# Feed-forward layers of a hybrid decoder: gated features kept in their accumulator copies, one tile in place of four, and earlier first loads for summed weights

## The chip, the cores and the metric

One Trainium2 chip, one core. The metric is the device time of one execution in microseconds (us), the median of repeated runs. The core has a matmul engine (TensorE, called PE in the profile; its weight loads are PEld), a vector engine (VectorE, DVE), an activation engine (ScalarE, ACT), GpSimd (POOL, which here issues the accumulating DMAs) and SyncE (SP, which issues the plain DMA loads). Each engine runs its own queue in order.

## What is computed

512 tokens of width 1024 go through two layers, a gated-MLP mixer in the first and retention in the second, each followed by the same kind of feed-forward layer (hidden width 2816). The change touches the feed-forward layers and the order of some loads elsewhere:

```python
def swiglu(h, w_gu, w_down):
    a, b = jnp.split(h @ w_gu, 2, axis=-1)
    return (jax.nn.silu(a) * b) @ w_down

def reference(...):
    h = x
    for i in range(DEPTH):                       # DEPTH = 2
        hn = rmsnorm(h, mix_norm_g[i])
        h = h + (sgu_mixer(hn, ...) if i % 2 == 0 else retention(hn, ...))
        h = h + swiglu(rmsnorm(h, ffn_norm_g[i]), ffn_w_gu[i], ffn_w_down[i])
    return rmsnorm(h, final_norm_g)
```

## The kernel before

**Arithmetic.** Every float32 operand is split in a high and a low part, `h` and `l`, of the matmul's own type; a product is three matmuls (`three`, L243 to L246). ACT makes the high part of a weight tile (`high`, L213), DVE the low part (`low`, L220). So each weight tile of 128 by 1024 has three buffers in its life: `wr` (raw, from the DMA), `wh` and `wl`.

**Seven products.** Large matrix products are done in blocks of two by two with seven block products in place of eight (`seven`, L313). They are called P1, P7, P6, Q4, P5, P2 and P3; in the feed-forward units and in small down projections their order is `LATER`: P1, P7, P6, P2, P5, Q4, P3. Some need a sum of several weight blocks. A sum is made on DVE (`plus`, L364), or by the DMA: the first block is loaded by SP (`load`, L333), and the others are added to it in place by accumulating DMAs that POOL issues (`add`, L336). For products named in `dma` the whole sum is made so; for products in `onto` the last block is added to the finished tile of the product before.

**A feed-forward layer** (`feed_forward`, L1003). First `project_t("gl...")` makes the last two of the 22 feature tiles (gates and values) with plain products; `first_evac` (L1016) applies silu to the gates and multiplies by the values. Then five `unit`s make four feature tiles each. In a unit, ACT copies three accumulators out of PSUM: `s1` after P1, `y7` after P7, `u2` after P6 (`copy`, L1028). After P2 and Q4 the gates `s1` and `u2` are completed and go through silu; `product` (L1032) multiplies them by the values, `y7` and the accumulator of P3. The results of units 0 to 3 go to tiles `hq[u][0]` and `hq[u][1]` of their own; those of unit 4 go to four tiles `he`, whose third slice already holds the two features of `gl` since the beginning of the layer. Down projections follow: `dn_0` after units 0 and 1, `dn_1` after unit 4 (`into_x`, L494). Where a down projection is small (`dn_0`: 14 steps) P7 and P5 are in `dma`, Q4 is in `onto`; `dn_1` has 28 steps, P7 in `dma`, P6 and Q4 in `onto`.

**Buffers.** Nearly all tiles, raw weights, their parts and the features, come from one pool `gen` of `N_GEN = 38` buffers of equal size (`G`, L123). A load or a result that finds none free waits until the last reader of one has finished.

**Order.** `pipeline` (L89) calls the preparations of a job a fixed number of jobs ahead: plain loads `FETCH = 8`, sums on DVE `SUM = 7`, high parts `HIGH = 6`, low parts `PREP = 5`. For a sum made by DMA the accumulating DMAs go `ADD = 8` jobs ahead (`STEP = 3` more for each further block) and the first load `LOAD` jobs ahead of the first of them. One job of a down projection is 12 matmuls, one of a unit 24 shorter ones. A scheduler then lays the engines' queues out, by this order as priority, and gives out the buffers.

```python
            if p in dma:
                n = len(bs) - 1
                return [(ADD + STEP * (n - 1) + LOAD, first)] + [
                    (ADD + STEP * (n - 1 - i), lambda b=b: add(p, b, g, s, nk)) for i, b in enumerate(bs[1:])]
```

Of the kernel before, what the change touches and what calls it, by code (L numbers as in the profile page):

```python
# [8 lines left out]
F32 = mybir.dt.float32  # L9
F32R = mybir.dt.float32r  # L10
I32 = mybir.dt.int32
AF = mybir.ActivationFunctionType
ALU = mybir.AluOpType
PSUM = bass.MemoryType.PSUM

P = 128
# [10 lines left out]
FETCH = 8  # L27
ADD = 8
STEP = 3
LOAD = 2  # L30
HIGH = 6
SUM = 7
N_GEN = 38
# [75 lines left out]
def trunk(ctx, tc, x, positions, mix_g, ffn_g, fin_g, sgu_w_in, sgu_w_s, sgu_b_s, sgu_ln_g, sgu_ln_b,  # L109
          sgu_w_out, ret_w_in, ret_gn_g, ret_w_out, ffn_w_gu, ffn_w_down, invf, decay, out):  # L110
    nc = tc.nc
# [9 lines left out]
    H = T // 2  # L121

    def G(name, dtype=F32, shape=(P, 2, T)):  # L123
        return gen.tile(list(shape), dtype, tag="g", name=name)
# [188 lines left out]
    def seven(name, w, groups, c1, c2, A, evac, mid=None, look=3, turned=False, order=ORDER, dma=(), onto=()):  # L313
# [21 lines left out]
        def add(p, b, g, s, nk):  # L335
            nc.gpsimd.dma_start(raw[p, 0, g, s][:, 0:nk, :], source(b, g, s, nk), accum_op=ALU.add)  # L336

        def fetch(p, g, s, nk):
# [10 lines left out]
# [4 lines that stand above are left out]
# [90 lines left out]
    def rows(k0, n):  # L443

        return [(list(range(k0, k0 + n // 2)), list(range(k0 + n // 2, k0 + n)))]
# [295 lines left out]
    def xA(name):  # L741

        made = {}

        def qr(i, j):
            return XR[name, i][j]

        s1 = []

        def A(p, g=0, ask=False):  # L750
            if p in ("P1", "P2", "Q4"):
                i, j = {"P1": (0, 0), "P2": (0, 1), "Q4": (1, 1)}[p]
                return tuple(xn[q][:, 4 * j:4 * j + 4, i * H:(i + 1) * H] for q in "hl")
            if p not in made:
                sign = -1.0 if p in ("P5", "P3") else 1.0
                h, l = (G(f"x{p}{q}_{name}", F32R, (P, 4, H)) for q in "hl")
                if p == "P6":
                    A("P5")
                elif p == "P3":
                    A("P6")  # L760
                s = G(f"x{p}_{name}", F32, (P, 4, H)) if p in ("P7", "P5") else s1[0]
                if p == "P5":
                    s1.append(s)

                def total():
                    a, b, op = {"P7": (qr(0, 0), qr(1, 0), ALU.subtract), "P5": (qr(1, 0), qr(1, 1), ALU.subtract),
                                "P6": (s, qr(0, 0), ALU.subtract), "P3": (s, qr(0, 1), ALU.add)}[p]
                    nc.vector.tensor_tensor(s, a, b, op)

                def high():  # L770
                    nc.scalar.activation(h, s, AF.Copy, scale=sign)

                def low():
                    nc.vector.scalar_tensor_tensor(l, s, sign, f32(h), ALU.mult, ALU.subtract)
                made[p] = Chain(total, high, low), (h, l)
            chain, hl = made[p]
            if not ask:
                chain.finish()
            return hl
        return A  # L780
# [222 lines left out]
    def feed_forward(l, ready):  # L1003

        w = ffn_w_gu[l]
        hq = [[None, None] for _ in range(5)]
        he = []
        gates = [None] * 5

        def hidden(u, i):  # L1010
            gates[u].finish()
            return hq[u][i]

        xparts = xA(f"f{l}")

        def first_evac(ps):  # L1016
            sl = G(f"silu{l}_l")
            nc.scalar.activation(sl, ps[0], AF.Silu)
            he.extend([[G(f"he{l}_{a}_{i}", F32, (P, 4, H)) for i in range(2)] for a in range(2)])
            for a in range(2):  # L1020
                for i in range(2):
                    hs = slice(i * H, (i + 1) * H)
                    nc.vector.tensor_tensor(he[a][i][:, 2, :], sl[:, a, hs], ps[1][:, a, hs], ALU.mult)

        def unit(u, mid=None):
            st_ = {}

            def copy(key, src):  # L1028
                st_[key] = G(f"{key}_{l}_{u}", F32, (P, 4, H))
                nc.scalar.activation(st_[key], src, AF.Copy)  # L1030

            def product(i, r, g, parts):  # L1032
                for ms, part in parts:
                    dst = he[part][i][:, 0:2, :] if u == 4 else hq[u][i][:, ms, :]
                    nc.vector.scalar_tensor_tensor(dst, r[:, ms, :], -1.0, g[:, ms, :], ALU.mult, ALU.mult)

            def evac(p, acc, c):
                if p == "P7":
                    copy("y7", acc["Y"])
                    if u < 4:  # L1040
                        hq[u] = [G(f"h{l}_{u}_{i}", F32, (P, 4, H)) for i in range(2)]
                elif p == "P1":
                    copy("s1", acc["X"])
                elif p == "P6":
                    copy("u2", acc["X"])
                elif p in ("Q4", "P2"):
                    a, ps = (st_["u2"], acc["Y"]) if p == "Q4" else (st_["s1"], acc["Z"])
                    gates[u] = Chain(lambda: nc.vector.tensor_tensor(a, a, ps, ALU.add),
                          lambda: nc.scalar.activation(a, a, AF.Silu),
                          *([lambda: product(1, st_["y7"], a, [(slice(0, 2), 0), (slice(2, 4), 1)] if u == 4 else [(slice(0, 4), 0)])] if p == "Q4" else []))  # L1050
                elif p == "P5":
                    nc.vector.tensor_tensor(st_["y7"], st_["y7"], acc["X"], ALU.add)
                elif p == "P3":
                    product(0, acc["X"], st_["s1"], [(slice(2 * c, 2 * c + 2), c)])
            seven(f"gu{l}_{u}", w, rows(0, KD), u * T, FF + u * T, xparts, evac, mid, turned=True, order=LATER, dma=("P7",), onto=("Q4",))

        t = [list(range(4 * u, 4 * u + 4)) for u in range(5)]
        A = [combos(f"h{l}_0", lambda g, i, j: hidden(j, i), (4,)),
             combos(f"h{l}_1", lambda g, i, j: he[j][i][:, 0:3, :] if g else hidden(2 + j, i), (4, 3))]

        project_t(f"gl{l}", w, ((20 * P, 2 * P), (FF + 20 * P, 2 * P)), first_evac, halves=True,
                  mid={("h", 0): lambda: xparts("P5", ask=True), ("h", 1): lambda: xparts("P7", ask=True), ("h", 2): lambda: xparts("P6", ask=True),
                       ("h", 3): lambda: xparts("P3", ask=True)})
        unit(0)
        unit(1, {("P2", 1): lambda: A[0]("P1", 0, ask=True), ("P5", 0): lambda: A[0]("P7", 0, ask=True), ("P3", 1): lambda: A[0]("P6", 0, ask=True)})
        into_x(f"dn{l}_0", ffn_w_down[l], [(t[0], t[1])], A[0])
        unit(2, {**{(p, 0): turn_tables for p in LATER}, ("P3", 1): turn_tables} if l == 0 else None)
        unit(3)
        unit(4, {("P2", 1): lambda: A[1]("P1", 0, ask=True), ("P5", 0): lambda: A[1]("P7", 0, ask=True), ("P3", 1): lambda: A[1]("P6", 0, ask=True)})
        into_x(f"dn{l}_1", ffn_w_down[l], [(t[2], t[3]), ([16, 17, 20], [18, 19, 21])], A[1], ready, look=5)  # L1070


    feed_forward(0, normed("r", mix_g[1:2], raw_copy("r")))

    xparts = xA("r")
# [147 lines left out]


    feed_forward(1, finish)
    pipeline(jobs)

# [32 lines left out]
```

## Time and profile before

| what | value |
| --- | --- |
| median of 3 runs | 1236.56 us (1231.20 to 1238.92) |
| the profiled execution's own time | 1234.63 us |
| its span, first to last instruction | 1232.7 us |
| granted TensorE clock, mean | 0.994 |
| PE / DVE / ACT / POOL busy | 1198.5 / 919.9 / 629.2 / 137.5 us |
| DMA | 204.87 MB, mean 166 GB/s |

The profile is of one execution; 1.9 us of its time lie outside the span. Busy time says how full an engine is, not whether it sets the end: for that the waits, the chain of work that ended last and the windows are read.

### The profile page before, as it was taken

To read this page: it belongs to the slowest core of one execution; us is meant where nothing else is said; L and a number is where in the kernel's file an instruction comes from. 1 tells how busy PE (TensorE), PEld (TensorE's weight loads), DVE (VectorE), ACT (ScalarE), POOL (GpSimd) and SP (SyncE) were. 2 spreads that over 40 slices of the span, in tenths; PEclk is the share of its full clock that TensorE was granted. 3 is DMA by queue.
4 is the path that set the end of the run, shared out by engine and by line. 5 is a ranking of instruction groups with operands and counts; after the bars stand their busy time and mean duration, and the time that the engine had idled before them with its cause. 6 is when DMAs were issued, how large, how long until landed. Compare 5 with 4: busy or idle time off the path is not lost.

```text
span 1232.7 us, 18012 instructions
## 1 busy us (share of the span) xinstructions
PE 1198.5 (97%) x7230; PEld 1071.5 (87%) x7230; DVE 919.9 (75%) x1105; ACT 629.2 (51%) x782; POOL 137.5 (11%) x125
## 2 busy tenths in 40 slices
PE   8999999998999999999999999999999989999996
PEld 7888899996999987888888888887899979999875
DVE  6385587687987698996665757779786778666887
ACT  7323365444544546655454646556654554455454
POOL 1000001111101120101101011220001011100310
PEclk9999999999999999999999999999999999999999
DMA  9323327678867987566566467896556678677982
GB/s 336 109 69 102 95 69 188 165 162 204 197 149 178 230 166 254 153 153 169 130 167 132 128 167 153 178 192 216 137 137 148 178 206 201 155 190 191 173 236 84
DMA packets 112995, 204.87 MB, mean 166 GB/s; under 512 B 7144, under 2 KB 20496, under 8 KB 112912
## 3 DMA queue, kind: packets, MB, share of 16 engines
q1 hardware_dynamic: 83088, 146.56, 37.0%
q0 software_dynamic: 29824, 57.18, 28.4%
q8 instruction: 56, 0.92, 0.3%
q14 instruction: 27, 0.22, 0.1%
HBM read 201.61 MB, written 2.10 MB: 165 GB/s over the span
## 4 chain that ended last, share of the span: by engine, by line
PE 83%; DMA 6%; DVE 5%; issue 3%; POOL 1%; ACT 1%; SPq 0%; DVEq 0%; POOLq 0%; ACTq 0%
PE X_gu L245 6%; PE X_gu L246 6%; PE X_gu L244 6%; DMA wr_dn_P<-in_ffn_w_down 4%; PE Y_gu L245 3%; PE Y_gu L244 3%; PE Y_gu L246 3%; PE X_vg L244 2%; PE X_vg L245 2%; PE ps_qk L246 2%; PE ps_qk L245 2%; PE ps_qk L244 2%; PE X_vg L246 2%; PE X_dn L245 2%; PE X_dn L244 2%
## 5 line engine op out<-in xcount | busy, mean ns | idle before, releaser
L213 ACT ACTIVATE wh_gu_P<-wr_gu_P 128x1024 fp32r<-128x1024 f32 x120 | 124.2, 1054 | 83.5 <-DMA wr_gu_P<-in_ffn_w_gu 33.8
L220 DVE TENSOR_TENSOR wl_gu_P<-wr_gu_P,wh_gu_P 128x1024 fp32r<-128x1024 f32 x120 | 145.2, 1219 | 21.2 <-ACT wh_gu_P L213 21.0
L213 ACT ACTIVATE wh_dn_P<-wr_dn_P 128x1024 fp32r<-128x1024 f32 x72 | 69.4, 982 | 71.5 <-DMA wr_dn_P<-in_ffn_w_down 37.6
L336 POOL DMA_DIRECT2D wr_gu_P<-in_ffn_w_gu x40 | 48.2, 1237 | 478.4 <-DMA wr_gu_P<-in_ffn_w_gu 148.0
L220 DVE TENSOR_TENSOR wl_dn_P<-wr_dn_P,wh_dn_P 128x1024 fp32r<-128x1024 f32 x72 | 79.8, 1128 | 14.4 <-ACT wh_dn_P L213 11.7
L220 DVE TENSOR_TENSOR wl_vg_P<-wr_vg_P,wh_vg_P 128x1024 fp32r<-128x1024 f32 x48 | 58.2, 1219 | 24.9 <-ACT wh_vg_P L213 19.9
L364 DVE TENSOR_TENSOR wr_gu_P<-wr_gu_P,wr_gu_P 128x1024 f32<-128x1024 f32 x40 | 48.6, 1221 | 31.2 <-DMA wr_gu_P<-in_ffn_w_gu 30.9
L336 POOL DMA_DIRECT2D wr_dn_P<-in_ffn_w_down x36 | 41.5, 1210 | 183.3 <-DVE wl_dn_P L220 78.5
L213 ACT ACTIVATE wh_vg_P<-wr_vg_P 128x1024 fp32r<-128x1024 f32 x48 | 49.7, 1055 | 20.1 <-PE X_vg L245 10.7
L336 POOL DMA_DIRECT2D wr_vg_P<-in_ret_w_in x24 | 28.9, 1294 | 265.6 <-DVE wl_qk L220 58.3
L244 PE MATMUL ps_qk<-XH_r,wh_qk 128*128 128x512 f32 (+1 forms) x160 | 55.3, 349 | 0.5 <-ACT XH_r L706 0.5
L245 PE MATMUL ps_qk<-XL_r,wh_qk 128*128 128x512 f32 (+1 forms) x160 | 55.5, 348 | 0.0
L246 PE MATMUL ps_qk<-XH_r,wl_qk 128*128 128x512 f32 (+1 forms) x160 | 55.3, 348 | 0.0
L244 PE MATMUL X_gu<-XH_f,wh_gu_P 128*128 128x256 f32 x160 | 45.4, 284 | 0.5 <-ACT xr_f L738 0.5
L245 PE MATMUL X_gu<-XL_f,wh_gu_P 128*128 128x256 f32 x160 | 45.3, 283 | 0.0
L246 PE MATMUL X_gu<-xP6h_f,wl_gu_P 128*128 128x256 f32 x160 | 45.3, 283 | 0.0
L245 PE MATMUL X_gu<-xP5l_f,wh_gu_P 128*128 128x256 f32 x160 | 45.3, 283 | 0.0
L245 PE MATMUL X_gu<-xP6l_f,wh_gu_P 128*128 128x256 f32 x160 | 45.3, 283 | 0.0
L244 PE MATMUL X_gu<-xP5h_f,wh_gu_P 128*128 128x256 f32 x160 | 45.3, 283 | 0.0
L246 PE MATMUL Y_gu<-XH_f,wl_gu_Q 128*128 128x256 f32 x160 | 45.3, 283 | 0.0
L246 PE MATMUL X_gu<-XH_f,wl_gu_P 128*128 128x256 f32 x160 | 45.3, 283 | 0.0
L244 PE MATMUL Z_gu<-XH_f,wh_gu_P 128*128 128x256 f32 x160 | 45.3, 283 | 0.0
(513 smaller groups left out, 4193.3 us busy)
## 6 DMA issues: line engine op xcount, KB each, us to landing
wr_gu_P<-in_ffn_w_gu SPq DMA_DIRECT2D x100, 512.0 KB, 4.5
wr_dn_P<-in_ffn_w_down SPq DMA_DIRECT2D x50, 512.0 KB, 5.3
wr_gu_P<-in_ffn_w_gu POOLq DMA_DIRECT2D x40, 512.0 KB, 6.8
wr_vg_P<-in_ret_w_in SPq DMA_DIRECT2D x40, 512.0 KB, 4.5
wr_dn_P<-in_ffn_w_down POOLq DMA_DIRECT2D x30, 512.0 KB, 7.6
wr_vg_P<-in_ret_w_in POOLq DMA_DIRECT2D x24, 512.0 KB, 6.3
wr_ro_P<-in_ret_w_out SPq DMA_DIRECT2D x20, 512.0 KB, 4.7
wr_qk<-in_ret_w_in SPq DMA_DIRECT2D x32, 256.0 KB, 3.1
```

The lines of the kernel that those rows point to most:

```text
L213: nc.scalar.activation(h, s, AF.Copy)
L220: nc.vector.tensor_tensor(l, s, f32(h), ALU.subtract)
L244: nc.tensor.matmul(o, ah, bh, start=start, stop=False, skip_group_check=True)
L245: nc.tensor.matmul(o, ah, bl, start=False, stop=False, skip_group_check=True)
L246: nc.tensor.matmul(o, al, bh, start=False, stop=stop, skip_group_check=True)
L336: nc.gpsimd.dma_start(raw[p, 0, g, s][:, 0:nk, :], source(b, g, s, nk), accum_op=ALU.add)
L364: nc.vector.tensor_tensor(a, a, b, ALU.add)
```

## The change

Three edits. `LOAD` goes from 2 to 3: the first load of every sum that the DMA makes goes out three jobs ahead of its first accumulating DMA. The results of units 0 to 3 are written over `y7` and `s1`, so `hq` has no tiles of its own. And `first_evac` writes one tile `hf` with a single multiply; the four `he` tiles are made only after P5 of unit 4 (`gather`), where ACT copies four slices of `hf` into them.

```diff
-LOAD = 2
+LOAD = 3
@@ feed_forward
+        first = []
         def first_evac(ps):
             sl = G(f"silu{l}_l")
             nc.scalar.activation(sl, ps[0], AF.Silu)
+            e = G(f"hf{l}")
+            nc.vector.tensor_tensor(e, sl, ps[1], ALU.mult)
+            first.append(e)
+
+        def gather():
+
             he.extend([[G(f"he{l}_{a}_{i}", F32, (P, 4, H)) for i in range(2)] for a in range(2)])
             for a in range(2):
                 for i in range(2):
-                    hs = slice(i * H, (i + 1) * H)
-                    nc.vector.tensor_tensor(he[a][i][:, 2, :], sl[:, a, hs], ps[1][:, a, hs], ALU.mult)
+                    nc.scalar.activation(he[a][i][:, 2, :], first[0][:, a, i * H:(i + 1) * H], AF.Copy)
@@ unit, evac
                 if p == "P7":
                     copy("y7", acc["Y"])
-                    if u < 4:
-                        hq[u] = [G(f"h{l}_{u}_{i}", F32, (P, 4, H)) for i in range(2)]
+                    hq[u][1] = st_["y7"]
                 elif p == "P1":
                     copy("s1", acc["X"])
+                    hq[u][0] = st_["s1"]
...
                 elif p == "P5":
                     nc.vector.tensor_tensor(st_["y7"], st_["y7"], acc["X"], ALU.add)
+                    if u == 4:
+                        gather()
```

## Rows read from the trace of the kernel before

**Rows 1.** The page's first part: busy time, share, instructions of each engine.

```profile
PE 1198.5 (97%) x7230; PEld 1071.5 (87%) x7230; DVE 919.9 (75%) x1105; ACT 629.2 (51%) x782; POOL 137.5 (11%) x125
```

**Rows 2.** Waits of PE, whole span: total us, times, longest.

```profile
PE Y_dn L244 <- ACT h_Q4h L479: 9.1, 2, 4.8
PE X_dn L245 <- DVE wl_dn_P L220: 2.9, 4, 0.9
...
PE X_ro L244 <- ACT z_P5h L479: 2.6, 1, 2.6
```

**Rows 3.** Windows: busy PE, PEld, DVE, ACT, POOL, granted clock, DMA share, GB/s.

```profile
290.80:296.80 6.00, 6.00 (x20) 4.67 (x21) 6.00 (x6) 4.81 (x5) 1.19 (x1) 0.73 0.87 310
...
1013.70:1019.70 6.00, 5.88 (x18) 4.43 (x19) 6.00 (x6) 4.60 (x5) 1.19 (x1) 0.72 0.94 314
...
464.00:478.00 14.00, 11.07 (x45) 8.34 (x46) 12.99 (x14) 9.56 (x15) 0.00 (x0) 1.00 0.76 252
1180.00:1201.00 21.00, 18.79 (x80) 14.60 (x79) 16.61 (x17) 10.88 (x16) 0.00 (x0) 1.00 0.90 267
520.00:820.00 300.00, 300.00 (x1426) 252.26 (x1425) 214.06 (x261) 162.90 (x224) 39.70 (x33) 1.00 0.65 150
```

**Rows 4.** The chain that ended last, first layer's `dn_0`: start, us, what.

```profile
266.10 0.23 PE X_dn L244
...
267.23 8.04 DMA wr_dn_P<-in_ffn_w_down
...
276.86 9.02 DMA wr_dn_P<-in_ffn_w_down
```

**Rows 5.** Timeline of ACT in `dn_0` of either layer.

```profile
285.91 1.06 ACT L213 ACTIVATE wh_dn_P<-wr_dn_P 128x1024 fp32r<-128x1024 f32 x1 [8.22 <-DMA wr_dn_P<-in_ffn_w_down]
...
1008.79 1.06 ACT L213 ACTIVATE wh_dn_P<-wr_dn_P 128x1024 fp32r<-128x1024 f32 x1 [8.73 <-DMA wr_dn_P<-in_ffn_w_down]
```

**Rows 6.** Waits of the SP queue, 243 to 270 us.

```profile
SPq L333 <- DVE wr_dn_P L364: 16.9, 2, 13.7
...
SPq L333 <- PE X_dn L246: 4.0, 1, 4.0
```

**Rows 7.** Timeline of the SP queue, end of its long wait.

```profile
258.62 0.37 SPq L333 DMA_DIRECT2D wr_dn_P<-in_ffn_w_down  x1
```

**Rows 8.** DMA, 243 to 262 us: busy tenths in 40 slices; issues, median us to landing.

```profile
DMA  0000769899999999970294999970000000137992
...
wr_dn_P<-in_ffn_w_down POOLq DMA_DIRECT2D x2, 512.0 KB, 6.5
```

**Rows 9.** Groups by shape: busy us, mean ns of one, idle before.

```profile
L1035 DVE SCALAR_TENSOR_TENSOR h<-y,u 128x1024 f32<-128x1024 f32 x8 | 9.8, 1224 | 9.3 <-ACT u L1049 5.6 <-PE X_dn L245 3.7
...
L1023 DVE TENSOR_TENSOR he<-silu_l,ps_gl 128x256 f32<-128x256 f32 x8 | 2.9, 416 | 2.4 <-PE ps_gl L246 1.3 <-ACT silu_l L1018 1.1
...
L1048 DVE TENSOR_TENSOR u<-u,Y_gu 128x1024 f32<-128x1024 f32 x10 | 12.1, 1214 | 0.0
...
L1131 ACT ACTIVATE sh<-s 128x256 fp32r<-128x256 f32 x4 | 1.6, 400 | 0.0
```

**Rows 10.** Waits of the SP queue, 400 to 432 us.

```profile
SPq L333 <- DVE wl_dn_P L220: 24.9, 1, 24.9
```

**Rows 11.** Timelines around `dn_1` of the first layer: ACT, POOL, DVE, PE.

```profile
427.87 1.06 ACT L213 ACTIVATE wh_dn_P<-wr_dn_P 128x1024 fp32r<-128x1024 f32 x1 [6.00 <-DMA wr_dn_P<-in_ffn_w_down]
...
425.82 1.19 POOL L336 DMA_DIRECT2D wr_dn_P<-in_ffn_w_down  x1 [3.78 <-DMA wr_dn_P<-in_ffn_w_down]
...
452.75 1.82 DVE L220 TENSOR_TENSOR wl_dn_P<-wr_dn_P,wh_dn_P 128x1024 fp32r<-128x1024 f32 x2
...
454.77 0.39 PE L245 MATMUL X_dn<-wl_dn_P,h_P6h 128*128 128x512 f32 x1
```

**Rows 12.** Timelines in the first retention head: DVE, then PE.

```profile
538.53 1.22 DVE L220 TENSOR_TENSOR wl_vg_P<-wr_vg_P,wh_vg_P 128x1024 fp32r<-128x1024 f32 x1
...
542.72 0.39 PE L245 MATMUL X_vg<-wl_vg_P,xP6h_r 128*128 128x512 f32 x1
```

## The prediction

> **What bounds the kernel now.** I read the page's busy times first: PE is busy 97% of the span [rows 1]. Of the 1232.7 us, 34.2 are left, so this edit of buffers and loads can only win PE's idle time, and what the clock loses after it. The waits of PE say where that is [rows 2]: the two longest, 9.1 us together, are in `dn_0`, one in each layer; then come small ones in `dn_1` (2.9 in four pieces), one in the retention's output projection (2.6) and the start. Between 520 and 820 us, the retention heads, PE has no idle time [rows 3].
>
> Next, what ends the long wait. The chain through `dn_0` of the first layer [rows 4] runs: SP issues a load at 267.23 that lands after 8.04 us; POOL's accumulating DMA onto it goes out at 276.86 and takes 9.02; ACT, which stood idle 8.22 us for exactly that landing [rows 5], makes the high part of this P5 weight, then those of Q4, then `h_Q4h`, and PE starts again. The second layer does the same (8.73 us on ACT [rows 5]). So PE waits for a sum that started too late. Why late: SP's queue had stood 13.7 us on one buffer whose last reader was a DVE sum [rows 6], until 258.62 [rows 7], and then 4.0 us more on one that a PE product of the same stage held [rows 6]. From 243 to 262 us the DMA engines have nearly empty stretches [rows 8]: there is bandwidth, there are no buffers. The pool of 38 is the bound behind the bound.
>
> After each of these waits PE runs for a while at the lower of its two clock levels: the granted clock is 0.73 over 6.0 us in one layer, 0.72 in the other [rows 3], a mean of the half level (1.2 GHz) and the full one (2.4 GHz). That loses (1 - 0.73) x 6 + (1 - 0.72) x 6 = 3.3 us. After the small waits of `dn_1` the clock stays 1.00 [rows 3].
>
> **The change, part by part.**
>
> *One tile `hf` in place of four `he`.* From the end of `gl` to P5 of unit 4, so through units 0 to 3 and `dn_0`, three more buffers are free. SP takes whatever is free for the next load in its queue. Before, the loads behind the 13.7 us wait are P2's first, P5's first, P2's second and P5's second (the late one, fourth). With three more buffers, three of them need not wait for the releases that they waited for.
>
> *`LOAD` 3.* The P5 and P7 loads move up one job, 12 x 0.23 = 2.7 us in a down projection [rows 4]; the adds stay at 8 jobs. In SP's order the second P5 load passes the second P2 load, so the late load becomes the third of the four, and the three new buffers reach it. It can then leave between the start and the end of that long wait, 244.9 to 258.6 us, in place of 267.23. Even at 258.6, with the 8.04 and 9.02 us of [rows 4] and 1.6 us between, its sum is complete at 277.3, 8.6 us ahead of 276.86 + 9.02 = 285.88. That is more than the 4.8 us that PE waited. I count both waits and both spells of low clock as gone: 9.1 + 3.3 = 12.4 us.
>
> *Results over `y7` and `s1`.* No instruction is added or removed. The two tiles live on as features where two new ones did, so what is saved is one buffer for the time of a product, and the wait for it: DVE stood idle 3.7 us in two places before `h<-y,u` for a buffer that a PE product of `dn_0` held [rows 9]. Neither wait reaches PE; it goes at zero, with 3.7 us as its upper end if DVE is late in `dn_0` afterwards.
>
> *What it adds.* In `first_evac`, four multiplies of 0.416 us become one, by the nearest shape (PSUM source, 1024 wide) 1.21 us [rows 9]: 0.45 us less on DVE in each layer, worth nothing at a point with no PE wait. In `gather`, four ACT copies of 256 columns, 0.40 us each by a copy of the same size [rows 9]: 1.6 us of ACT in each layer, beside the last products of unit 4, where ACT stands idle 6.00 us for a landing [rows 11]. Hidden; uncovered it would be 2 x 1.6 = 3.2 us. Its other price is buffers: four at once, while SP already waits 24.9 us for one [rows 10]. Behind a copy that waits stand ACT's high parts for `dn_1`, and behind those DVE and PE. Bounds: nothing, if the scheduler finds four released together; the rival below, if not. I take nothing net, since P7's loads for `dn_1` also leave earlier, and their adds go out as soon as they land (POOL [rows 11]).
>
> *`LOAD` elsewhere.* In each unit and retention head a P7 load now stands ahead of P1's first in SP's queue. Where buffers are short that costs P1 one turn; in the units the three buffers pay for it, in the heads nothing does. The tightest head weight I found has 542.72 - (538.53 + 1.22) = 3.0 us between its low part and its use [rows 12], about one job. I take 0; the bounds are a gain of the 2.6 us of the output projection [rows 2] and a loss of one job less that margin in four heads, near 0, or 2.7 in one if it has no margin.
>
> *What is late next.* With the wait gone, DVE's work in `dn_0` is pressed into less time, as in `dn_1`, where PE loses 2.9 and 2.2 us in small pieces [rows 3]. `dn_0` has half the steps and fewer sums in a row; I take 0.5 us a layer, 1.0 in all, with 0 and 5.1 as ends.
>
> Sum: 12.4 - 1.0 = 11.4 us. The profiled execution took 1234.63 us, so its like would take 1223.2; the median of the runs is 1.93 higher, so 1236.56 - 11.4 = 1225.2: I say **1225**.
>
> **The rivals.**
>
> *The buffers go elsewhere.* High and low parts and feature parts ask for buffers too. If they take the three, only the one job of `LOAD` is left: 4.8 - 2.7 and 4.3 - 2.7 remain, 3.7 us, without low clock: 12.4 - 3.7 = 8.7 us, 1228. If the scheduler's order on POOL also puts the two Q4 adds ahead, the whole wait may stay: 1236. Middle 1231. For it: SP's waits show a pool that is never free. Against: SP takes a load as soon as one is.
>
> *More than forecast.* The earlier P7 sums start the sequence P7, P6, Q4 of `dn_1` sooner, and its 2.9 + 2.2 us go as well: 1236.56 - 12.4 - 5.1 = 1219. For it: the adds follow the landing of the loads [rows 11]. Against: DVE is busy 12.99 of 14 us there [rows 3].
>
> *Earlier loads slow the adds.* Accumulating DMAs of the same size land in 6.5 us in a window with empty stretches [rows 8] and in 9.02 beside more loads [rows 4]. If the loads that moved up sit beside P7's adds, these land 2.5 us later. `dn_0` bears that; in `dn_1` DVE ends a pair of low parts at 454.57 and PE uses the first at 454.77 [rows 11], 0.8 us after that first one ended, so 1.7 us would show in each layer: 1225 + 3.4, about 1229. The Trainium skill, "DMA: Bandwidth & Descriptors", section "Issuing engines are not separate DMA queues", speaks for this rival: DMAs started by different engines run on the same 16 DMA engines and interleave, so an earlier start on one queue is paid by the other. By that rule the trace agrees that adds slow down in company, but the empty stretches of [rows 8] are where the loads would move to.
>
> *Slower than before: `gather` holds ACT.* The four copies sit in ACT's queue at P5 of unit 4 and wait for buffers while three early loads that nobody needs yet hold theirs. SP's wait there was 24.9 us for one buffer [rows 10]; if ACT waits half of that, 12 us, less 2 us of margin (0.8 in the tightest place, 3 elsewhere), PE loses 10 us in each layer and the low clock comes back there, 3.3: 23.3 - 12.4 gives 1247. It decides from 12.4 / 2 + 2 = 8 us of wait a layer. Against it: these copies come earlier in the program than the later loads of `dn_1`, and so go before them where a buffer is given out.
>
> **How the numbers follow.** Forecast 0.48 (1225, its own range 1220 to 1229); buffers elsewhere 0.24 (1228 to 1236); more than forecast 0.15 (1219); adds slowed 0.04 (1229); `gather` 0.09 (1240 to 1250). About 1% (12.4 us) is what a measurement of this kernel can tell from no change; by chance the terms of the sum come to just that. Faster by more needs under 1224.2: the 1219 case and some four tenths of the forecast, 0.35. Slower by more needs over 1248.9: half of the last rival, 0.05. The rest 0.60. The range 1218 to 1237 leaves out most of the last rival and the edge of the 1219 case, under 2 in 10.
>
> **What would show it.** In the profile after: the two waits of PE before `Y_dn` gone from its list and no clock below 1.00 in `dn_0`; SP's load for the second P5 sum leaving before 260 us and its add landing before PE reaches P2's end; ACT idle before that high part under 2 us; `dn_1`'s waits still near 2.9 and 2.2. If PE still waits in `dn_0` for the same landing, the buffers went elsewhere; if waits appear on ACT before the copies of `hf`, and on PE at the start of `dn_1`, `gather` took the gain. The forecast is wrong above all if the scheduler lays the queues out in a way that the old trace doesn't suggest, since every queue is laid out anew.

## The result, and the profile after

| | median us | runs | range | profiled execution, its span |
|---|---|---|---|---|
| before | 1235.32 | 6 | 1231.20 to 1238.92 | 1234.63, 1232.7 |
| after | 1220.03 | 6 | 1218.24 to 1221.26 | 1218.24, 1216.5 |

The ratio is 0.9879, with a 95% interval of 0.9855 to 0.9903: 15.3 us less by the medians, 16.2 by the two spans, where 11.4 were forecast. The time lies within the range given. Of the three chances it is "faster by over 1%" that the median falls into (the interval just reaches across), the case that had been given 0.35.

First the page's busy times and PE's waits over the whole span, which answer [rows 1] and [rows 2]:

```profile
PE 1192.5 (98%) x7230; PEld 1068.3 (88%) x7230; DVE 919.7 (76%) x1099; ACT 629.6 (52%) x790; POOL 137.4 (11%) x125
```

```profile
PE X_dn L245 <- DVE wl_dn_P L220: 3.1, 4, 1.1
PE X_ro L244 <- ACT z_P5h L479: 2.7, 1, 2.7
```

The 9.1 us before `Y_dn` are no longer in the list. What is left in the forecast's places is DVE's low parts in `dn_1` and the retention's output projection, which kept its 2.7. Where the time came from is seen from three windows, one a stage: first layer's FFN, retention with its output projection, second layer's FFN. Before, then after (length, then PE's busy time and the other engines'):

```profile
157.60:500.30 342.70, 334.37 (x2359) 313.84 (x2358) 278.86 (x305) 177.55 (x200) 44.45 (x38) 1.00 0.72 180
500.30:872.10 371.80, 368.07 (x1787) 310.26 (x1786) 277.70 (x343) 207.37 (x287) 43.37 (x37) 1.00 0.66 163
872.10:1224.00 351.90, 342.34 (x2375) 319.60 (x2373) 266.14 (x279) 178.33 (x201) 42.67 (x37) 0.99 0.68 168
```

```profile
157.20:491.50 334.30, 332.03 (x2358) 312.93 (x2357) 278.65 (x302) 177.57 (x204) 44.71 (x38) 1.00 0.73 185
491.50:863.50 372.00, 368.18 (x1787) 310.33 (x1786) 278.32 (x343) 207.66 (x287) 43.22 (x36) 1.00 0.66 162
863.50:1207.90 344.40, 340.05 (x2375) 318.76 (x2373) 265.20 (x277) 178.37 (x205) 42.40 (x36) 1.00 0.68 171
```

The retention is as long as it was. The two FFNs are 8.4 and 7.5 us shorter, in two ways: PE's idle time (length less busy time) falls from 8.3 to 2.3 and from 9.6 to 4.4, 11.3 together; and PE's busy time, for the same matmuls, falls by 2.3 in each, 4.6 together. The second is for the most part the clock (3.5 of the 4.6, worked out further down): in either layer one spell at the lower level is gone, as the windows over `dn_0` show (they answer the first two of [rows 3]; the sixth number is the granted clock), with `dn_1` of either layer under them:

```profile
283.80:289.80 6.00, 6.00 (x29) 4.95 (x28) 6.00 (x7) 3.19 (x3) 1.99 (x2) 1.00 1.01 240
1001.00:1007.00 6.00, 6.00 (x28) 4.96 (x27) 5.11 (x5) 3.07 (x3) 1.71 (x2) 1.00 0.88 157
450.00:464.00 14.00, 12.90 (x57) 10.17 (x56) 10.32 (x11) 5.50 (x6) 0.00 (x0) 1.00 0.94 279
1162.00:1183.00 21.00, 20.12 (x88) 15.98 (x86) 17.12 (x17) 10.89 (x15) 1.55 (x2) 1.00 0.92 271
```

In six microseconds of `dn_0` PE now does 29 matmuls where it did 20. In `dn_1` PE's single waits add up to 1.6 us in the first layer and 1.4 in the second, where they were 2.9 and 2.2: the ones before `Y_dn` are gone there as well.

Now the chain that the forecast was about, on its three queues in the first layer's `dn_0`. SP's waits from 243 to 270 us answer [rows 6], and the load of P5's second sum [rows 4]; then POOL's accumulating DMAs and ACT, which answer [rows 4] and [rows 5]:

```profile
SPq L333 <- DVE h_P7l L483: 10.8, 1, 10.8
SPq L333 <- PE Y_gu L246: 5.6, 1, 5.6
SPq L333 <- DVE y L1041: 3.6, 1, 3.6
```

```profile
258.43 0.76 SPq L333 DMA_DIRECT2D wr_dn_P<-in_ffn_w_down  x1
```

```profile
256.33 1.19 POOL L336 DMA_DIRECT2D wr_dn_P<-in_ffn_w_down  x1 [12.24 <-DMA wr_dn_P<-in_ffn_w_down]
265.38 1.22 POOL L336 DMA_DIRECT2D wr_dn_P<-in_ffn_w_down  x1 [7.86 <-DVE h_S L457]
267.10 2.43 POOL L336 DMA_DIRECT2D wr_dn_P<-in_ffn_w_down  x2 [0.51 <-issue]
```

```profile
272.66 1.99 ACT L213 ACTIVATE wh_dn_P<-wr_dn_P 128x1024 fp32r<-128x1024 f32 x2
274.55 1.04 ACT L479 ACTIVATE h_P5h<-h_S 128x1024 fp32r<-128x1024 f32 x1
275.50 1.04 ACT L213 ACTIVATE wh_dn_Q<-wr_dn_P 128x1024 fp32r<-128x1024 f32 x1
278.01 1.07 ACT L213 ACTIVATE wh_dn_Q<-wr_dn_P 128x1024 fp32r<-128x1024 f32 x1 [1.47 <-DMA wr_dn_P<-in_ffn_w_down]
278.98 1.04 ACT L479 ACTIVATE h_Q4h<-y 128x1024 fp32r<-128x1024 f32 x1
```

The load leaves at 258.43 instead of 267.23. Its add goes out at 265.38, is complete at 272.85 and makes nobody wait: both high parts of P5 follow each other at 272.66. `h_Q4h` is ready at 280.0, where it was ready at 290.8. Two things are not as forecast. SP's longest wait is still 10.8 us where it was 13.7, though the first load behind it leaves at 252.07 where it was 258.62. And POOL's queue has another order: P5's second add now stands ahead of the two adds of Q4 (the pair at 267.10), where it stood behind them.

### The profile page after: what moved, and what is told of

Same layout as the page of the kernel before. It is cut to its first block, busy times and chain, and to the rows that moved or that the text cites. A ratio compares the mean times of both kernels' runs of the same rounds, so it can differ in the third digit from the quotient of the medians.

```text
span 1216.5 us, 18009 instructions
## 1 busy us (share of the span) xinstructions
PE 1192.5 (98%) x7230; PEld 1068.3 (88%) x7230; DVE 919.7 (76%) x1099; ACT 629.6 (52%) x790; POOL 137.4 (11%) x125
## 4 chain that ended last, share of the span: by engine, by line
PE 87%; DVE 4%; issue 3%; DMA 3%; POOL 1%; ACT 1%; SPq 0%; DVEq 0%; POOLq 0%; ACTq 0%
PE X_gu L246 6%; PE X_gu L245 6%; PE X_gu L244 6%; PE Y_gu L246 3%; PE Y_gu L244 3%; PE Y_gu L245 3%; PE X_vg L244 2%; PE ps_qk L246 2%; PE ps_qk L245 2%; PE X_vg L246 2%; PE X_vg L245 2%; PE ps_qk L244 2%; PE X_dn L245 2%; PE X_dn L246 2%; PE X_dn L244 2%
## 5 line engine op out<-in xcount | busy, mean ns | idle before, releaser
L220 DVE TENSOR_TENSOR wl_gu_P<-wr_gu_P,wh_gu_P 128x1024 fp32r<-128x1024 f32 x120 | 144.9, 1219 | 38.7 <-ACT wh_gu_P L213 38.6
L220 DVE TENSOR_TENSOR wl_vg_P<-wr_vg_P,wh_vg_P 128x1024 fp32r<-128x1024 f32 x48 | 58.2, 1219 | 25.9 <-ACT wh_vg_P L213 20.7
L336 POOL DMA_DIRECT2D wr_vg_P<-in_ret_w_in x24 | 28.8, 1219 | 265.0 <-DVE sl L1140 59.7
L220 DVE TENSOR_TENSOR wl_gu_Q<-wr_gu_P,wh_gu_Q 128x1024 fp32r<-128x1024 f32 x20 | 24.4, 1222 | 28.9 <-ACT wh_gu_Q L213 28.9
L244 PE MATMUL Y_gu<-xP7h_f,wh_gu_P 128*128 128x256 f32 x160 | 45.3, 283 | 0.0
L245 PE MATMUL Y_gu<-xP7l_f,wh_gu_P 128*128 128x256 f32 x160 | 45.3, 283 | 0.0
L246 PE MATMUL Y_gu<-xP7h_f,wl_gu_P 128*128 128x256 f32 x160 | 45.3, 283 | 0.0
L244 PE MATMUL X_gu<-xP6h_f,wh_gu_P 128*128 128x256 f32 x160 | 45.3, 283 | 0.0
```

Source lines behind the costliest of these rows:

```text
L220: nc.vector.tensor_tensor(l, s, f32(h), ALU.subtract)
L244: nc.tensor.matmul(o, ah, bh, start=start, stop=False, skip_group_check=True)
L245: nc.tensor.matmul(o, ah, bl, start=False, stop=False, skip_group_check=True)
L246: nc.tensor.matmul(o, al, bh, start=False, stop=stop, skip_group_check=True)
```

## The experiments

Each run has its time and ratio against the kernel before on the same chip. Totals hide which stage moved, so the table also has the lengths of three stages in the profiled execution: from the first `ps_gl` to the first `ps_qk`, from there to the second layer's first `ps_gl`, and from there to PE's last instruction. Between 371.8 and 373.8 in the middle column only a spell of low clock or a small wait around the output projection differs. In the last column most executions have such a spell near 890 us, at the stage's start, and five of those with `hf` have none (LOAD 2, add three jobs late, not in place, P5's add held, 37 buffers); it makes 1.5 us (PE's busy time from there to `dn_0` is 110.3 us with it and 108.8 without).

| kernel | median us | ratio (95%) | FFN 1 | retention | FFN 2 |
|---|---|---|---|---|---|
| before | 1235.32 | 1 | 342.7 | 371.8 | 351.9 |
| after | 1220.03 | 0.9879 (0.9855 to 0.9903) | 334.4 | 372.0 | 344.4 |
| LOAD 3 only | 1223.84 | 0.9900 (0.9880 to 0.9919) | 336.0 | 373.1 | 346.8 |
| hf and gather only | 1225.47 | 0.9919 (0.9899 to 0.9939) | 339.3 | 371.9 | 350.7 |
| in place only | 1232.17 | 0.9969 (0.9956 to 0.9983) | 340.5 | 373.1 | 350.4 |
| after, LOAD 2 | 1223.58 | 0.9903 (0.9883 to 0.9924) | 335.8 | 373.3 | 344.3 |
| LOAD 3 for P5 only | 1224.74 | 0.9913 (0.9899 to 0.9926) | 337.3 | 373.1 | 346.3 |
| LOAD 3, add three jobs late | 1234.34 | 0.9987 (0.9973 to 1.0000) | 341.6 | 376.6 | 346.5 |
| after, add three jobs late | 1223.15 | 0.9898 (0.9883 to 0.9913) | 337.0 | 374.6 | 344.5 |
| after, not in place | 1220.03 | 0.9875 (0.9860 to 0.9889) | 335.5 | 373.1 | 344.4 |
| LOAD 3, P5's add held behind Q4's | 1229.44 | 0.9961 (0.9947 to 0.9975) | 336.4 | 378.5 | 347.0 |
| after, P5's add held behind Q4's | 1226.54 | 0.9937 (0.9922 to 0.9953) | 335.5 | 378.1 | 345.2 |
| after, LOAD 4 | 1224.90 | 0.9920 (0.9904 to 0.9936) | 335.4 | 377.3 | 345.0 |
| after, 37 buffers | 1220.72 | 0.9902 (0.9884 to 0.9921) | 334.5 | 373.8 | 343.6 |

**LOAD 3 only.** The theory: the waits in `dn_0` are a lack of buffers, and both the three buffers and the early load are needed.

```diff
-LOAD = 2
+LOAD = 3
```

> The kernel before with LOAD 3 and nothing else. Theory (the long wait in dn_0 is a lack of buffers, and the early load only shortens it): P5's second load moves up one job, 2.7 us, so of the waits of 4.8 and 4.3 us before Y_dn some 2.1 and 1.6 stay, and the clock after them stays at its full level or not: 1226 to 1232 us against 1235 for the kernel before. Rival A (the order of the loads alone does it, because the late load goes out third instead of fourth): both waits gone, as in the changed kernel, 1220 to 1223. Rival B (without buffers an earlier place in the queue brings nothing, SP stands at the same buffer): the waits stay at 4 to 5 us each, 1234 to 1238.

1223.84 us: one line brings 12.4 of the 14.9 us (by ratio), near rival A's time. SP's longest wait is still 13.9 us, and the first two loads behind it leave at 258.56 and 262.38, where it was 258.62 and 262.32. P5's second load left at 264.08, 3.15 us earlier, as the third of the four; the fourth left at 267.03. The place alone does not make these 3 us: in the kernel before the third of the four left at 266.81, only 0.4 us ahead of the fourth. Both times the third waited for a buffer that a product of `dn_0` held, and here it found one 2.7 us sooner, the length of one job. Why the new layout had one for it was not looked into. PE's wait before `Y_dn` is not gone but 1.3 and 1.0 us. Compare ACT's work behind the last landing, before (what follows the row at 285.91 in [rows 5]) and with LOAD 3:

```profile
286.87 1.04 ACT L479 ACTIVATE h_P5h<-h_S 128x1024 fp32r<-128x1024 f32 x1
287.82 1.99 ACT L213 ACTIVATE wh_dn_Q<-wr_dn_P 128x1024 fp32r<-128x1024 f32 x2
289.71 1.04 ACT L479 ACTIVATE h_Q4h<-h 128x1024 fp32r<-128x1024 f32 x1
```

```profile
278.94 1.06 ACT L213 ACTIVATE wh_dn_P<-wr_dn_P 128x1024 fp32r<-128x1024 f32 x1 [1.56 <-DMA wr_dn_P<-in_ffn_w_down]
...
285.49 1.06 ACT L213 ACTIVATE wh_dn_Q<-wr_dn_P 128x1024 fp32r<-128x1024 f32 x1 [2.31 <-DMA wr_dn_P<-in_ffn_w_down]
286.45 1.04 ACT L479 ACTIVATE h_Q4h<-h 128x1024 fp32r<-128x1024 f32 x1
```

The last add lands at 285.40, hardly sooner than the 285.88 of before. But it is now Q4's add that is last, and behind it ACT has one high part and `h_Q4h` to make (until 287.5) instead of five instructions (until 290.8). That looks as if the new order on POOL were the gain; the runs on the order below test it.

**hf and gather only.**

```diff
+            e = G(f"hf{l}")
+            nc.vector.tensor_tensor(e, sl, ps[1], ALU.mult)
...
+                    nc.scalar.activation(he[a][i][:, 2, :], first[0][:, a, i * H:(i + 1) * H], AF.Copy)
```

> The kernel before with one tile hf in place of the four he until unit 4, and the gather; LOAD stays 2, the features keep their own tiles. Theory (buffers): three more free buffers take away SP's wait of 13.7 us in dn_0, the load for P5's second sum leaves before 262 us and both long waits of PE are gone: 1220 to 1225 us, a gain of 11 to 15. Rival (the early load is what counts): the late load is still the fourth behind the wait, one more than the three buffers, and at least 3 us of each wait stay: 1229 to 1236. If the gather cost anything, ACT would stand idle before its four copies and PE at the start of dn_1, and the time would be above 1236.

1225.47 us, just above the theory's time, but not in its way. SP's long wait is still 13.5 us; P5's second load left only 1.7 us earlier (265.54) and its sum was complete at 283.00 instead of 285.88. A new wait took part of it, as the list of PE's waits and ACT's timeline show:

```profile
PE X_gu L244 <- ACT wh_gu_P L213: 4.2, 2, 2.1
...
PE Y_dn L244 <- ACT h_Q4h L479: 1.7, 2, 1.0
```

```profile
283.08 1.06 ACT L213 ACTIVATE wh_dn_P<-wr_dn_P 128x1024 fp32r<-128x1024 f32 x1 [7.09 <-DMA wr_dn_P<-in_ffn_w_down]
284.05 1.04 ACT L479 ACTIVATE h_P5h<-h_S 128x1024 fp32r<-128x1024 f32 x1
285.00 1.99 ACT L213 ACTIVATE wh_dn_Q<-wr_dn_P 128x1024 fp32r<-128x1024 f32 x2
286.89 1.04 ACT L479 ACTIVATE h_Q4h<-h 128x1024 fp32r<-128x1024 f32 x1
287.84 1.99 ACT L213 ACTIVATE wh_dn_P<-wr_dn_P 128x1024 fp32r<-128x1024 f32 x2
289.73 1.04 ACT L213 ACTIVATE wh_gu_P<-wr_gu_P 128x1024 fp32r<-128x1024 f32 x1
```

After the landing ACT works off a train of high parts without a gap, and the next unit's first weight stands at its end: PE gets `h_Q4h`, does Q4, and waits 2.1 us for `wh_gu_P`. In the changed kernel that high part is made at 284.14. The profiled execution took 1230.43 us, the longest of the six, so the waits in it are more than the median run can have had; both spells of low clock are still in it (0.72 over six microseconds from 290.7 and from 1010.4). Nor does this run part the buffers from the copies on ACT: the kernel before with more buffers and nothing else was not run.

**In place only.**

```diff
-                    if u < 4:
-                        hq[u] = [G(f"h{l}_{u}_{i}", F32, (P, 4, H)) for i in range(2)]
+                    hq[u][1] = st_["y7"]
```

> The kernel before with the features written over y7 and s1, LOAD 2, four he as before. Theory (as predicted: worth nothing by itself, it frees two buffers for the length of a product only): 1233 to 1237 us, the waits of dn_0 stay at 4 to 5 us each. Rival (the gain of the changed kernel came from here, because two more buffers per unit let the loads of dn_0 run ahead): 1220 to 1226, both waits gone or under 1 us. A gain in between, 1227 to 1232, would say that the buffers of the features are a part of the sum that was left out.

1232.17 us, 3.8 less by the ratio: between the two. The waits before `Y_dn` are 3.4 and 3.1 us, 2.6 less together. The load leaves 0.8 us earlier and its add takes 7.65 instead of 9.02. So the edit that was put at zero has a value of its own, and it lies in the same wait.

**The changed kernel with LOAD 2**, and **without the features in place.**

> The changed kernel with LOAD back at 2: hf, the gather and the features in place stay. Theory (buffers): the long waits in dn_0 stay away and most of the gain with them, 1219 to 1224 us; the two smaller waits before Y_dn in dn_1, which the changed kernel lost as well, come back if it was the earlier P7 load that took them away (about 1.3 and 0.8 us, so 1222 to 1223). Rival (LOAD 3 makes the gain, the buffers only allow it): waits of 2 us or more come back in dn_0 and the time is 1228 to 1236.

> The changed kernel without the features in place: hf, the gather and LOAD 3, with two tiles for every unit's features as before. By itself the edit in place brought 4.3 us, where it had been predicted at nothing. Theory (it only shortens a wait that the other two parts take away as well, so it is worth nothing beside them): 1219 to 1222, no wait in dn_0. Rival (its buffers are a part of the sum of their own, in dn_1 and the units too): 1223 to 1226, with PE's waits in dn_1 or in dn_0 longer by 2 us or more in all.

LOAD 2: 1223.58 us, a ratio of 0.9903 against 0.9879, so LOAD 3 is worth about 3 us beside the other parts, though the intervals overlap. There is no wait before `Y_dn`, but the new one before `X_gu` is there with 1.5 and 1.2 us. The two waits of `dn_1` before `Y_dn` did not come back, so they don't hang on LOAD alone. Without the features in place: 1220.03 us and 0.9875, the same as the whole change. Its 3.8 us are in the wait that the other two parts take away as well; the small waits of `dn_1` before `Y_dn` are back (1.8 us in all in this trace).

**LOAD 3 for P5 alone.**

```diff
-LOAD = 2
+LOAD = {"P5": 3, "P7": 2}
```

> The kernel before with LOAD 3 for the loads of P5 alone (only down projections have them); those of P7 stay at 2. Theory (what counts is that the load for P5's second sum goes out third instead of fourth behind SP's long wait): the waits of PE before Y_dn in dn_0 fall from 4.8 and 4.3 to under 2 us each as with LOAD 3 for both (1.3 and 1.0), and 9 to 12 us of the 12.7 come: 1224 to 1228 against 1236.5. Rival (the early loads of P7 in every unit do it, by letting all of DVE and ACT run ahead): the waits of dn_0 stay over 3 us and the time is 1231 to 1237. The small waits before Y_dn in dn_1 (0.75 and 0.77 in the first layer) should come back if P7's place took them away.

1224.74 us, waits in `dn_0` of 0.8 and 1.6 us: the P5 loads alone bring nearly all that LOAD brings. Against LOAD 3 for both (0.9900) the P7 loads may be worth 1.6 us, inside the intervals. The waits before `Y_dn` in the first layer's `dn_1` are back (0.6 and 0.8), as was expected if the earlier place of P7's loads took them away. But that place is not all there is to them: they are gone with LOAD 2 and back in the changed kernel without the features in place.

**The order on POOL, first attempt.** The add is put out three jobs later.

```diff
-                    (ADD + STEP * (n - 1 - i), ...
+                    (ADD - 3 * (p == "P5" and s > 0) + STEP * (n - 1 - i), ...
```

> The kernel before with LOAD 3, and the add of P5's second sum put out three jobs later, so that POOL's queue holds it behind the two adds of Q4, as in the kernel before; with LOAD 3 alone it stands ahead of them. SP's loads have the same order as with LOAD 3 alone. Theory A (the earlier landing of the load is the gain): the add goes out right behind Q4's, at about 272 to 273 us, lands near 281, ACT needs the 4.9 us behind it that it needed before, and PE waits 0 to 2 us: 1222 to 1227. Theory B (the order on POOL is the gain: with P5's add ahead, only Q4's last high part is left behind the last landing): the waits are back at 3 to 5 us and the time at 1230 to 1236.

> The changed kernel with the add of P5's second sum three jobs later, behind Q4's two adds on POOL as in the kernel before. Theory A (the load's time counts): its load leaves near 258 us as in the changed kernel, the add goes out near 269, lands by 279, and PE finds everything ready: 1219 to 1222, no wait in dn_0. Theory B (the order on POOL counts): waits of 2 us or more before Y_dn or before the next unit's first product, 1225 to 1231.

1234.34 us, by the total theory B, and 1223.15, between the two theories. The trace says something else. Three jobs later is behind the high part of the same weight, so the add had to wait for ACT to read it; the high part holds the first block alone and the second goes into the low part (the same sum, rounded otherwise). First of the two kernels, ACT and POOL:

```profile
274.99 1.99 ACT L213 ACTIVATE wh_dn_P<-wr_dn_P 128x1024 fp32r<-128x1024 f32 x2
```

```profile
277.38 1.20 POOL L336 DMA_DIRECT2D wr_dn_P<-in_ffn_w_down  x1 [5.71 <-ACT wh_dn_P L213]
```

The add lands at 286.91, DVE's low part waits for it, and PE waits 4.1 us for DVE's `h_P5l` behind that. The same edit costs a wait of 2.1 us in a retention head. Neither run tests the order.

**The order on POOL, second attempt**, with an order of issue only.

```diff
+            with tc.issue_after(q4[-1]) if p == "P5" and s > 0 and q4 else nullcontext():
+                i = nc.gpsimd.dma_start(raw[p, 0, g, s][:, 0:nk, :], source(b, g, s, nk), accum_op=ALU.add)
+            if p == "P6" and b == BLOCKS["Q4"][-1] and s > 0:
+                q4.append(i.ins)
```

> The kernel before with LOAD 3, and POOL's queue held to the order of the kernel before: P5's second add behind the two adds of Q4 (an order of issue only, no wait; with LOAD 3 alone it stands ahead of them). This replaces the run that put the add three jobs later, where the add came to wait for ACT's high part of the same weight and so showed nothing of the order. Theory A (the earlier load is the gain): its load leaves near 264 us, lands by 272.5, the add goes out at once since POOL is free by then, lands near 281, ACT's chain behind it takes the 4.9 us of the kernel before, and PE, due near 286, waits 0 to 1.5 us: 1222 to 1226, as with LOAD 3 alone (1223.8). Theory B (the order on POOL is the gain, because less work of ACT stands behind the last landing): waits of 3 us or more before Y_dn in both layers, 1228 to 1235.

> The changed kernel with POOL's queue held to the order of the kernel before, P5's second add behind the two of Q4. Theory A (with the load landed by 265 us the order is of no matter): the add goes out near 269, lands by 279, no wait before Y_dn: 1219 to 1222. Theory B (the order is part of the gain): waits of 1 us or more before Y_dn or behind it, 1223 to 1229.

1229.44 and 1226.54 us, and again the totals say theory B. The stages don't. The FFNs are nearly as long as without the edit: 336.4 and 347.0 against 336.0 and 346.8 with LOAD 3; 335.5 and 345.2 against 334.4 and 344.4, where small waits of `dn_1` are back. The loss is in the retention, 5.3 and 6.2 us, because `seven` is called for the retention heads' `vg` too and the edit holds P5's add back there as well. The kernel with LOAD 3: PE's waits, the stage's window without and with the edit up to the output projection, and ACT and POOL in the first head:

```profile
PE Y_dn L244 <- ACT h_Q4h L483: 3.4, 2, 2.5
...
PE sc L244 <- ACT k0h L1096: 3.1, 1, 3.1
```

```profile
493.75:778.41 284.66, 283.66 (x1400) 240.63 (x1399) 203.57 (x252) 152.98 (x207) 30.02 (x25) 1.00 0.61 150
```

```profile
494.22:785.38 291.16, 287.08 (x1401) 242.51 (x1400) 203.84 (x252) 153.36 (x207) 29.55 (x25) 0.99 0.59 148
```

```profile
545.64 1.06 ACT L213 ACTIVATE wh_vg_P<-wr_vg_P 128x1024 fp32r<-128x1024 f32 x1 [8.39 <-DMA wr_vg_P<-in_ret_w_in]
```

```profile
534.37 2.44 POOL L338 DMA_DIRECT2D wr_vg_P<-in_ret_w_in  x2 [17.45 <-DVE wl_vg_P L220]
```

Held behind Q4's add, P5's goes out at 535.10 and lands at 545.62; ACT stands idle 8.39 us for it, PE 3.1, and the low clock behind that makes PE's busy time 3.4 us longer. But this is not the order of the kernel before. In its first head three adds go out from 521.71 on, P5's two among them, and the one left over at 540.40 is Q4's: the high part that waits for its landing is `wh_vg_Q`.

```profile
521.71 3.64 POOL L336 DMA_DIRECT2D wr_vg_P<-in_ret_w_in  x3 [21.16 <-DVE wl_vg_P L220]
540.40 1.22 POOL L336 DMA_DIRECT2D wr_vg_P<-in_ret_w_in  x1 [15.05 <-ACT wh_vg_P L213]
```

```profile
549.47 1.06 ACT L213 ACTIVATE wh_vg_Q<-wr_vg_P 128x1024 fp32r<-128x1024 f32 x1 [2.73 <-DMA wr_vg_P<-in_ret_w_in]
```

So the edit made an order there that neither kernel had, and the 6.5 and 5.0 us that the heads lost are its price; the rest of the 5.3 and 6.2 is a spell of low clock at the output projection, which one execution of each pair has. In `dn_0`, where the question was, the waits before `Y_dn` are 0.9 and 2.5 us in the old order against 1.3 and 1.0 in the new; in the changed kernel there is none in either order. So in `dn_0` theory A holds: the earlier load is the gain (with the old order P5's second sum is complete at 282.25 instead of 285.88), and the order on POOL is worth nothing in the first layer and 1.5 us at most in the second.

**LOAD 4, and 37 buffers**, each in the changed kernel.

> The changed kernel with LOAD 4: the summed loads a further job (2.7 us in a down projection) ahead, P7's both ahead of P1's. Theory (dn_0 has no wait left, and what is left in dn_1, 3.1 us, is DVE's low parts, not loads): nothing to gain, 1218 to 1222; as the early loads hold buffers longer, a loss up to 3 us is possible, 1220 to 1223. Rival (the places in dn_1 and the output projection still hang on loads): 2 us or more better, below 1218.

> The changed kernel with 37 buffers in the pool in place of 38. Theory (the pool is the bound behind the bound, as the prediction put it, and the gain hangs on three buffers more): one buffer less gives back about a third of what buffers brought, SP's waits in dn_0 get longer by some 2 us and waits come back before Y_dn or behind it: 1222 to 1228. Rival (the earlier place of the loads brings the gain and there are buffers to spare): 1219 to 1222, no wait in dn_0. A loss of more than 10 us would say that another stage needs all 38.

LOAD 4 takes 1224.90 us, a loss larger than the theory's. The FFNs are within 1.1 us of the changed kernel's, so this earlier place gained nothing there; the loss, 5.4 us, is in the retention stage, where PE's order of products at the output projection came out otherwise. PE waits for its features, 2.0 us more in all, and its busy time is 3.3 us longer, with a mean granted clock of 0.99 over the stage where it was 1.00:

```profile
PE X_ro L244 <- ACT z_P6h L479: 3.3, 1, 3.3
...
PE Y_ro L244 <- ACT z_Q4h L479: 1.2, 1, 1.2
```

Which of the early loads brought that order about was not tried. With 37 buffers: 1220.72 us, 0.9902, and no wait in `dn_0`. SP's longest wait there is 15.3 us, longer than before the change, and still the load leaves near 259.7:

```profile
SPq L333 <- PE Y_gu L246: 17.9, 2, 15.3
```

The intervals of 0.9902 and 0.9879 overlap; in the trace 1.9 us went in the retention, as busy time of PE (370.1 us against 368.1) and not as waits, and PE's idle time in the two FFNs grew by 0.9. One buffer fewer is thus of little matter; it does not say what three are worth. No kernel tried is faster than the changed one; the one without the features in place equals it.

## Why the prediction was right, and what in it was not

- **Where the time is.** Right: both FFNs give it, the retention nothing, and the waits in `dn_0` go with the low clock behind them. The list of what would show it held for `dn_0`: no wait before `Y_dn`, clock 1.00, the load out before 260 us, its sum complete at 272.85 (277.3 was forecast for the latest start), ACT not waiting for it. Its line on `dn_1` did not: single waits of 1.6 and 1.4 us are left there, not 2.9 and 2.2.
- **The terms of the sum.** Waits of `dn_0`: 9.1 forecast, 9.3 gone (with a piece of 0.12 behind them). Low clock: 3.3 forecast, 3.5 measured on the same 24 matmuls from the wait's end on. In the first layer they took 7.06 us before and take 5.44 now, from the first to the second row of each pair:

```profile
290.81 0.80 PE L244 MATMUL Y_dn<-wh_dn_Q,h_Q4h 128*128 128x512 f32 x1 [4.80 <-ACT h_Q4h L479]
297.87 0.39 PE L245 MATMUL X_dn<-wl_dn_P,h_P5h 128*128 128x512 f32 x1
```

```profile
285.46 0.39 PE L244 MATMUL Y_dn<-wh_dn_Q,h_Q4h 128*128 128x512 f32 x1
290.90 0.39 PE L245 MATMUL X_dn<-wl_dn_P,h_P5h 128*128 128x512 f32 x1
```

  In the second layer it is 7.31 (without the piece of 0.12) and 5.44. The other 1.1 us by which PE's busy time fell are not the clock; kernels that have no spell in the first FFN differ in it by as much (332.0 to 333.1), and what makes it stays open. "What is late next", -1.0: nothing came late in `dn_0` in the changed kernel. It did in the kernels with half of the change: 2.1 us a layer before `X_gu` with hf alone. `dn_1`: 0 forecast, 2.1 gone; no run shows which part takes them away. 9.3 + 3.5 + 1.1 + 2.1 = 16.0 against 11.4; the two spans differ by 16.2. So the place and the two large terms were right to 0.2 us each. What the sum lacked, the waits of `dn_1`, the loss that did not come and the 1.1 us, all lay to the same side.
- **How the two parts act.** Here the working was wrong. It needed three buffers *and* the earlier place, buffers to end SP's long wait and the place to come within their reach. For the moment at which the load leaves both do count: 267.23 before, 265.54 with hf only, 264.08 with LOAD 3 only, 258.43 in the changed kernel. But PE had waited less than 5 us, and for it either part is nearly enough alone: 10.0 and 12.4 us of the 14.9. Nor did SP's wait have to end: it is 10.8 us after the change, 13.9 with LOAD 3 alone, 15.3 with 37 buffers and no wait of PE. The rival "the buffers go elsewhere" did not come true, since the load leaves 5.65 us sooner than with LOAD 3 alone; and it had that case too dear: it gave the one job of LOAD 2.7 us of each wait, and it took away 3.4 to 3.5.
- **One wait, three ways out.** Alone, the parts bring 12.4, 10.0 and 3.8 us by the ratios, 26 in all; together 14.9. Each takes from the same wait, and it goes once. In place was put at zero with 3.7 us as its upper end, for a wait of DVE; alone it is worth 3.8, by another way (the load leaves 0.8 us earlier), and beside the others nothing.
- **"More than forecast"** gave 1219 by all of `dn_1`'s waits going. That the time came out beside it is luck: `dn_1` gave only 2.1 of its 5.1; the rest is the 1.0 us that was not lost, the 1.1 of busy time, and a median of the kernel before that is 1.2 us lower over six runs than over the three of the forecast.
- **`gather` holds ACT.** It doesn't. ACT makes the four copies in a row, with no idle time before them:

```profile
407.61 1.32 ACT L1029 ACTIVATE he<-hf 128x256 f32<-128x256 f32 x4
```

  Their price is on SP instead, which waits 5.3 us for the buffer of `hf` until they have read it, and nobody waits for that load. The multiply in `first_evac` took 1.22 us, as forecast.
- **Earlier loads slow the adds.** In `dn_0` they didn't: P5's two adds and then Q4's two took 10.0, 9.0, 9.2 and 10.9 us before, and 5.7, 7.5, 8.3 and 9.9 after. Adds do slow down in company: one that ran alone took 6.0 us (at 174.6 in the kernel before), the three in a row at 273.08 with LOAD 3 took 5.8, 8.2 and 10.9. With this agrees the rule of the Trainium skill that the prediction cited ("DMA: Bandwidth & Descriptors", section "Issuing engines are not separate DMA queues"), as far as the sharing of DMA engines goes: all three came from POOL, so the row does not show DMAs of different issuing engines side by side. In the changed kernel ACT waits 1.5 us for Q4's last add (at 278.01), and PE does not wait.

## What to carry to other kernels

Where several edits feed one wait, measure each alone before adding up: the first to arrive takes the gain, and the next bottleneck (here ACT's train of high parts) decides what the rest is worth. For a load that is late behind a queue's long wait, count its place among the loads that leave when the wait ends; moving it up one job, from the fourth place to the third, brought as much here as a tile in place of four did (12.4 and 10.0 us, with overlapping intervals). And compare stages before believing a total: an edit in a helper reaches every stage that calls it, and twice here the total pointed to a cause in `dn_0` while the loss was in a retention head, in an order of issue that the kernel before did not have.

## What had not been expected of the hardware

PE's wait of 2.6 to 2.9 us in the output projection is the same in nearly every kernel, yet a spell at the lower clock follows it in some executions (that of LOAD 3 only: granted clock 0.98 from the projection's first matmul to the second layer's first `ps_gl`, PE busy 85.8 us) and not in others (the kernel before: 1.00 and 84.4 us). The wait alone doesn't decide it, and a difference of 1.3 us between two executions can be this and nothing else. And a stage's busy time is no measure of a spell: it fell by 2.3 us a layer here, where the same matmuls take 1.6 and 1.9 us less, close to what the granted clock over six microseconds gave (1.62 and 1.68).
